# Moving modulation loads and half of the query and key stores to other DMA queues in a two-layer transformer kernel

## The chip, the cores and the metric

The kernel runs on one core of one Trainium2 chip. The metric is device time in microseconds (us). The kernel before took 3096.09 us, the median of 3 runs (3091.0 to 3099.82). The core has five engines that run side by side, each with its own instruction queue in a fixed order: TensorE (PE, matrix products; its weight loads are shown as PEld), VectorE (DVE), ScalarE (ACT), GpSimd (POOL) and SyncE (SP). A transfer between memory and the core's on-chip buffers is issued by an instruction in one of these queues and then runs by itself; an instruction that needs its data waits for it on a semaphore, and everything behind that instruction on the same engine waits too.

## The reference

Two transformer layers over 1024 tokens and 256 context tokens of width 1024, in float32. Only the beginning of the first layer matters here:

```
mod   = silu(c)     @ mod_w[0] + mod_b[0]      # 6 x 1024 numbers: shifts, scales and gates
mod_c = silu(c_ctx) @ mod_w[0] + mod_b[0]
xn = rms_norm(h,  norm1_g) * (1 + sc1)  + sh1
cn = rms_norm(hc, norm1_g) * (1 + csc1) + csh1
aq, ak, av, bq, bk, bv = split(xn @ w_in)      # the same for cn
aq, ak, bq, bk = apply_rope(...)               # pairs (x1, x2) -> (x1 cos - x2 sin, x1 sin + x2 cos)
```

Attention, a convolutional feed-forward network, and a second layer with gated linear attention follow. The shifts sh2, scales sc2 and gates g1, g2 of layer 0 are not needed before the attention's output.

## The kernel before

Products in float32 are made of three products of split operands: `split` (L104) writes the rounded high part with ScalarE (`wh`, L110) and the rest with VectorE (`wl`, L90, the line of the helper `tt`).

The stage that is changed is `attn_in` (from L344). After norming, the queries and keys are made in six pairs of projections: `part(w0)` gives the even channels E of 4 heads for all 1280 tokens, `part(w0 + 1)` the odd channels O. Each is 120 matrix products into one of the two accumulators `big`, so the next projection but one can't start before VectorE and ScalarE have emptied the accumulator. Emptying means: multiply with cosines and sines (`ec`, `es` for E; `os`, `oc` for O), and split the 256 context columns as they are (`shi`, `slo`, L110 and L90, 128x256). From the four products come the two rotated halves, which are split again (128x1024) and stored to DRAM as 4 blocks of 32 rows, 1280 columns each: four stores of 640 KB for a pair, a high and a low one for each rotated half. The stores are issued by GpSimd (L100, `dma2`). The tiles `shi` and `slo` have two buffers each, so a pair's context split waits for the stores of the pair before. The last key projection (`ks[2]`, L456 to L459) makes four stores of 2 blocks of 32 rows, 320 KB each.

Between the projections the rest of the modulation of layer 0 is worked in: 32 blocks of 128 rows of `mod_w` (transposed), 512 KB each. `mod_block` (L300) loads one into the tile `mraw` (two buffers here) and VectorE reduces it twice at L308, against the rows of silu(c) and silu(c_ctx), 1.2 us a pass (`junk` is the first pass, `mraw` the second). The load of a block can be issued once the block two before it has been reduced. `some_mod(n)` takes the next n blocks.

All loads are issued by SyncE (L96, `dma`): the modulation blocks as well as the weights (`wraw`, two buffers, 512 KB each). Three engines' orders are not written by hand in this stage: a scheduler puts the recorded instructions of each engine in one order by its own estimate of when each can run. So VectorE's order mixes emptying, weight splits (`wl`) and modulation passes, and it changes when a transfer moves to another queue.

Of the kernel before, what the change touches and what calls it, by code (L numbers as in the profile page):

```python
# [9 lines left out]
F32 = mybir.dt.float32  # L10
# [34 lines left out]
class K:  # L45
# [254 lines left out]
    def mod_block(self, pool, src, dst, rows):  # L300

        raw = pool.tile([P, 1024], F32, name="mraw", tag="mraw", bufs=self.mbufs)
        self.dma(raw, src)
        for v, row in enumerate(rows):
            out = raw
            if v < len(rows) - 1:
                out = pool.tile([P, 1024], mybir.dt.bfloat16, name="junk", tag="junk", bufs=1)
            self.nc.vector.tensor_tensor_reduce(out=out, in0=raw, in1=row, scale=1.0, scalar=0.0,  # L308
                                                op0=ALU.mult, op1=ALU.add, accum_out=dst[:, v:v + 1])
# [38 lines left out]
    def attn_in(self, esv):  # L348
        nc, io = self.nc, self.io
        with ExitStack() as esx:  # L350
            es0 = ExitStack()
            hp = self.pool(es0, "x0")
            x = [hp.tile([P, T], F32, name=f"x0{k}") for k in range(KD)]
            mp = self.pool(es0, "mod0")
            xp = self.pool(esx, "xn1", side="right")
            xh = [xp.tile([P, T], F32R, name=f"x1h{k}") for k in range(KD)]
            xl = [xp.tile([P, T], F32R, name=f"x1l{k}") for k in range(KD)]
            self.open_tmp()
            xs = lambda k, a, b: x[k][:, a:a + b]
            A, B = self.A[0][0], self.B[0][0]  # L360

            def load_x(t0, n):
                for k in range(KD):
                    self.dma(x[k][:, t0:t0 + n], io["xT"][k, :, t0:t0 + n])

            load_x(*MAIN0)
            self.mbufs = 3
            rows = self.mod_rows(xp, 2)
            y = self.rstd_rows(xs, *MAIN0, True)
            first = [self.mod_first(mp, rows, lambda: self.load_w(io["w_qk"][0])), self.load_w(io["w_qk"][1])]  # L370
            load_x(*MAIN1)
            for k in range(KD):
                self.norm_chunk(k, xs, xh, xl, *MAIN0, A[:, :, 0], B[:, :, 0], y)
            self.norm_mod(xs, xh, xl, *MAIN1, A[:, :, 0], B[:, :, 0], True)
            load_x(*CTX)
            self.norm_mod(xs, xh, xl, *CTX, A[:, :, 1], B[:, :, 1], True)
            self.close_tmp()
            es0.close()
            vp = self.pool(esv, "v")
            fh = lambda k, a, b: xh[k][:, a:a + b]  # L380
            fl = lambda k, a, b: xl[k][:, a:a + b]
            with ExitStack() as es1:
                rp = self.pool(es1, "rope")
                cos = rp.tile([P, NM], F32, name="cos")
                sin = rp.tile([P, NM], F32, name="sin")
                self.dma(cos, io["cos"])
                self.dma(sin, io["sin"])
                self.mbufs = 2
                mod = []

                def some_mod(n):
                    if not mod:
                        mod.append(self.mod_steps([(0, j) for j in (2, 3, 4, 5)], rows, rp))
                    for _ in range(n):
                        next(mod[0], None)

                def full(name, bufs):
                    return rp.tile([P, NM], F32, name=name, tag=name, bufs=bufs)

                def halves():  # L400
                    return [rp.tile([P, T], F32R, name="s" + a, tag="s" + a, bufs=2) for a in ("hi", "lo")]

                def part(j):
                    ps = self.big()
                    self.proj(ps, first[j] if j < 2 else self.load_w(io["w_qk"][j]), fh, fl, TALL)
                    return ps

                M, C = slice(0, NM), slice(NM, T)

                def pair(w0, scr):  # L410

                    def out(eo, t):
                        hi, lo = hl[eo]
                        self.split(hi[:, M], lo[:, M], t)
                        for half, y in ((0, hi), (1, lo)):
                            r = 64 * half + 32 * eo
                            self.dma2(scr[:, r:r + 32, :], y.bitcast(F32))
                    hl = [halves(), halves()]
                    E = part(w0)
                    ec, es, oc, os = (full(a, 1) for a in ("ec", "es", "oc", "os"))  # L420
                    self.tt(ec, E[:, M], cos, ALU.mult)
                    self.tt(es, E[:, M], sin, ALU.mult)
                    self.split(hl[0][0][:, C], hl[0][1][:, C], E[:, C])
                    some_mod(2)
                    O = part(w0 + 1)
                    self.tt(os, O[:, M], sin, ALU.mult)
                    self.tt(oc, O[:, M], cos, ALU.mult)
                    self.split(hl[1][0][:, C], hl[1][1][:, C], O[:, C])
                    self.tt(ec, ec, os, ALU.subtract)
                    out(0, ec)  # L430
                    self.tt(es, es, oc, ALU.add)
                    out(1, es)
                    some_mod(2)

                self.vA = vp.tile([P, 10, P], F32, name="vA")
                self.vB = [[vp.tile([P, 5, 256], F32, name=f"vB{g}{b}") for b in range(2)] for g in range(2)]

                def values(g):
                    self.proj_tok([io["w_v"][2 * g], io["w_v"][2 * g + 1]], fh, fl, self.vB[g], 10)
                    some_mod(2)  # L440
                for j in range(6):
                    pair(2 * j, self.qs[j] if j < 4 else self.ks[j - 4])
                    if j == 3:
                        values(0)

                E = part(12)
                hi, lo = halves()
                ec, es = full("ec", 1), full("es", 1)
                self.tt(ec, E[:, M], cos, ALU.mult)
                self.tt(es[0:64], E[64:128, M], sin[64:128], ALU.mult)  # L450
                self.tt(es[64:128], E[0:64, M], sin[0:64], ALU.mult)
                self.split(hi[:, C], lo[:, C], E[:, C])
                self.tt(ec[0:64], ec[0:64], es[0:64], ALU.subtract)
                self.tt(ec[64:128], ec[64:128], es[64:128], ALU.add)
                self.split(hi[:, M], lo[:, M], ec)
                for half, y in ((0, hi), (1, lo)):  # L456
                    for eo in range(2):
                        r = 64 * half + 32 * eo
                        self.dma2(self.ks[2][:, r:r + 32, :], y[64 * eo:64 * eo + 64].bitcast(F32))  # L459
                some_mod(4)  # L460

                E = part(13)
                vt = halves()[0].bitcast(F32)
                nc.scalar.copy(vt, E[:, :T])
                for b0, nb in ((0, 4), (4, 4), (8, 2)):
                    ps = self.sm()
                    for b in range(nb):
                        nc.tensor.transpose(out=ps[:, b * P:(b + 1) * P], in_=vt[:, (b0 + b) * P:(b0 + b + 1) * P],
                                            identity=self.ident)
                    nc.scalar.copy(self.vA[:, b0:b0 + nb, :], ps[:, :nb * P].rearrange("p (b e) -> p b e", e=P))  # L470
                self.attn_consts(vp)
                values(1)
                some_mod(48)

    def proj_tok(self, srcs, fh, fl, dst, nblk):

# [1357 lines left out]
```

## Time and profile before

| | |
|---|---|
| median of 3 runs | 3096.09 us (3091.0 to 3099.82) |
| profiled execution, its own time | 3087.69 us |
| its span | 3085.8 us |
| mean granted clock of TensorE | 0.982 of full speed |
| TensorE busy | 2931.9 us (95%) |
| VectorE busy | 2272.7 us (74%) |
| ScalarE busy | 1486.7 us (48%) |
| GpSimd busy | 82.7 us (3%) |

The profiled execution is 8.4 us under the median of the runs (0.27%), so a sum is made against 3087.69 us and the difference is carried over to the median. Busy shares are means over stages with different limits. The changed stage lies between 75 us and 330 us of the span, and what a change there is worth has to be read from that stretch.

### The profile page before, as it was taken

The page shows a single profiled execution, that of the slowest core. Times are in us where ns is not written, and L with a number is a line of the kernel's source. Part 1 is how long each engine was busy: PE and PEld are TensorE (multiplying, and loading weights), DVE is VectorE, ACT ScalarE, POOL GpSimd, SP SyncE. Part 2 cuts the span into 40 slices and gives each one's busy share as a digit, 9 for nine tenths or more (in the row PEclk, how much of TensorE's full clock was granted, in tenths as well). Part 3 has the DMA queues.
Part 4 walks back from the last instruction along what each step waited for, and adds up shares of the span by engine and source line. Part 5 has one row for each costly group of instructions (what it writes and reads, how often), then busy time and mean ns, then how long its engine had stood idle before and what let it go on. Part 6 is the DMA issues. An engine that isn't in the chain of part 4 may idle for free.

```text
span 3085.8 us, 41864 instructions
## 1 busy us (share of the span) xinstructions
PE 2931.9 (95%) x15758; PEld 2469.0 (80%) x15758; DVE 2272.7 (74%) x3805; ACT 1486.7 (48%) x2720; POOL 82.7 (3%) x148
## 2 busy tenths in 40 slices
PE   8888799999999999999998999999999899999997
PEld 4687789998898788887887888888877688887886
DVE  7666388887598888887876568688687988887454
ACT  5111277776466544445354355445454544445342
POOL 0000000000000000000000000000000000000000
PEclk9989899999999999999999999999999999999999
DMA  6664652211555322223856651111143222225552
GB/s 217 187 180 140 159 150 63 62 56 51 196 165 187 110 82 82 82 81 130 298 176 194 210 183 36 45 42 46 44 166 123 75 82 82 82 82 191 177 171 90
DMA packets 185443, 383.95 MB, mean 124 GB/s; under 512 B 28276, under 2 KB 89588, under 8 KB 185240
## 3 DMA queue, kind: packets, MB, share of 16 engines
q1 hardware_dynamic: 159032, 326.70, 33.2%
q0 software_dynamic: 25056, 52.48, 5.5%
q8 instruction: 124, 2.03, 0.3%
q10 hardware_dynamic: 1152, 2.10, 0.2%
q14 instruction: 79, 0.65, 0.1%
HBM read 311.44 MB, written 69.73 MB: 124 GB/s over the span
## 4 chain that ended last, share of the span: by engine, by line
PE 73%; DVE 10%; issue 7%; DMA 5%; ACT 4%; POOL 1%; SPq 0%; DVEq 0%; ACTq 0%; POOLq 0%
PE bk L1053 26%; PE bk L1138 16%; PE big L140 14%; DMA mraw<-in_mod_wt_dram 3%; PE sm L553 2%; PE sm L602 2%; PE sm L668 2%; PE big L487 2%; PE big L528 2%; PE sm L1635 2%; PE big L536 2%; PE sm L1566 1%; DVE F L90 1%; DMA wraw<-in_ffn_down_dram 1%; DVE wl L90 1%
## 5 line engine op out<-in xcount | busy, mean ns | idle before, releaser
L110 ACT CAST wh<-wraw 128x512 fp32r<-128x512 f32 x568 | 345.8, 619 | 699.4 <-PE bk L1138 205.4
L90 DVE TENSOR_TENSOR wl<-wraw,wh 128x512 fp32r<-128x512 f32 x568 | 387.9, 687 | 297.8 <-ACT wh L110 277.9
L1138 PE MATMUL bk<-dh,wh 128*128 128x512 f32 (+1 forms) x880 | 328.8, 374 | 15.3 <-ACT wh L110 10.9
L1138 PE MATMUL bk<-dl,wh 128*128 128x512 f32 (+1 forms) x880 | 326.9, 371 | 3.8 <-DVE dl L90 3.8
L1138 PE MATMUL bk<-dh,wl 128*128 128x512 f32 (+1 forms) x880 | 326.8, 371 | 0.2 <-DVE wl L90 0.2
L110 ACT CAST wh<-S 128x512 fp32r<-128x512 f32 x176 | 108.9, 621 | 225.6 <-DVE S L90 118.3
L1138 PEld LDWEIGHTS bk<-dh,wh 128*128 128x128 f32 x880 | 168.2, 191 | 46.8 <-ACT wh L110 11.7
L1138 PEld LDWEIGHTS bk<-dl,wh 128*128 128x128 f32 x880 | 168.3, 191 | 33.2 <-DVE dl L90 4.7
L1138 PEld LDWEIGHTS bk<-dh,wl 128*128 128x128 f32 x880 | 168.2, 191 | 28.3 <-DVE wl L90 0.9
L140 PE MATMUL big<-x1h,wh 128*128 128x512 f32 (+1 forms) x336 | 124.1, 372 | 23.5 <-DVE slo L90 22.5
L308 DVE CUSTOM_DVE_ANT_0 mraw<-mraw,crow 128x1024 f32<-128x1024 f32 x88 | 107.5, 1221 | 31.7 <-DMA mraw<-in_mod_wt_dram 30.6
L140 PE MATMUL big<-x1h,wl 128*128 128x512 f32 (+1 forms) x336 | 124.9, 372 | 5.9 <-DVE wl L90 5.9
L90 DVE TENSOR_TENSOR wl<-S,wh 128x512 fp32r<-128x512 f32 x176 | 120.1, 684 | 11.1 <-ACT wh L110 10.8
L140 PE MATMUL big<-x1l,wh 128*128 128x512 f32 (+1 forms) x336 | 124.3, 371 | 0.0
L87 DVE SCALAR_TENSOR_TENSOR h<-h,cw,h 128x1023 f32<-128x1023 f32 x88 | 111.0, 1279 | 17.9 <-ACT h L93 17.8
L87 DVE SCALAR_TENSOR_TENSOR hh<-hh,cw,hh 128x1023 f32<-128x1023 f32 x88 | 110.9, 1278 | 15.5 <-ACT hh L93 15.4
L560 ACT COPY wt<-sm 128x512 f32<-128x512 f32 (+1 forms) x196 | 95.7, 527 | 38.6 <-PE sm L553 38.2
L308 DVE CUSTOM_DVE_ANT_0 junk<-mraw,crow 128x1024 bf16<-128x1024 f32 x56 | 68.4, 1221 | 55.1 <-DMA mraw<-in_mod_wt_dram 54.8
L553 PE MATMUL sm<-ident,pt 128*128 128x128 f32 x672 | 103.7, 277 | 5.3 <-DVE oc L723 3.3
L584 DVE TENSOR_REDUCE nm<-big 128x1 f32<-128x1280 f32 x64 | 95.4, 1490 | 18.0 <-PE big L536 17.9
L140 PE MATMUL bk<-x2ch,wh 128*128 128x256 f32 x352 | 101.0, 287 | 3.9 <-ACT wh L110 3.0
L140 PE MATMUL big<-x3h,wh 128*128 128x512 f32 x256 | 103.9, 406 | 0.0
(468 smaller groups left out, 8249.4 us busy)
## 6 DMA issues: line engine op xcount, KB each, us to landing
wraw<-in_ffn_down_dram SPq DMA_DIRECT2D x110, 512.0 KB, 3.9
mraw<-in_mod_wt_dram SPq DMA_DIRECT2D x88, 512.0 KB, 4.3
wraw<-in_ffn_up_dram SPq DMA_DIRECT2D x88, 512.0 KB, 3.5
graw<-in_ffn_up_dram SPq DMA_DIRECT2D x44, 512.0 KB, 3.5
dx<-gs SPq DMA_DIRECT2D x88, 256.0 KB, 4.4
gs<-h POOLq DMA_DIRECT2D x22, 512.0 KB, 2.9
gs<-hh POOLq DMA_DIRECT2D x22, 512.0 KB, 2.9
q<-qs SPq DMA_DIRECT2D x40, 256.0 KB, 3.3
```

The lines of the kernel that those rows point to most:

```text
L87: return self.nc.vector.scalar_tensor_tensor(out=out, in0=in0, scalar=scalar, in1=in1, op0=op0, op1=op1)
L90: return self.nc.vector.tensor_tensor(out=out, in0=a, in1=b, op=op)
L110: self.nc.scalar.copy(hi, src)
L140: self.nc.tensor.matmul(ps[:, t0:t0 + n], self.columns(a, k * m, m), b(k, t0, n), start=(k == 0 and j == 0), stop=(k == KD - 1 and j == 2))
L308: self.nc.vector.tensor_tensor_reduce(out=out, in0=raw, in1=row, scale=1.0, scalar=0.0, op0=ALU.mult, op1=ALU.add, accum_out=dst[:, v:v + 1])
L487: self.nc.tensor.matmul(ps[:, 256 * b:256 * b + 256], a(k, t0, P), self.columns(w, k % 4 * 256, 256), start=(k == 0 and j == 0), stop=(k = ...
L528: nc.tensor.matmul(out, q[:, 0, s, :], key, start=True, stop=False)
L553: nc.tensor.transpose(out=ps[:, b * P:(b + 1) * P], in_=self.p[:, (b0 + b) * P:(b0 + b + 1) * P], identity=k.ident)
L560: copy(self.wt[:, b0 * P:(b0 + c) * P], self.tp[g][:, :c * P])
L584: nc.vector.tensor_reduce(out=nm, in_=self.S[m][:, :T], axis=AX.X, op=ALU.max, negate=True)
L1053: nc.tensor.matmul(ps, a[:, s], b, start=(start and k == 0 and j == 0), stop=(k == 3 and j == 2), skip_group_check=True)
L1138: nc.tensor.matmul(out(d), self.columns(a, d * P, P), b, start=(c == 0 and j == 0 and d % per == 0), stop=(c == NFF - 1 and j == 2), skip_ ...
```

## The change

Three transfers change their queue, in the stage between the opening of `rope` and the end of `attn_in` alone:

- the 32 loads of modulation blocks go from SyncE's queue to GpSimd's (`mod_dma2`, set after the sines and cosines are loaded, and unset at the end of the stage);
- the stores of the high parts `shi` (12 of 640 KB, 2 of 320 KB) go from GpSimd's queue to ScalarE's, each behind the ScalarE copy that made its data;
- the stores of the low parts `slo` stay in GpSimd's queue.

What is computed, the sizes of the transfers, the buffers and the memory layout stay as they are.

```
     def mod_block(self, pool, src, dst, rows):
         raw = pool.tile([P, 1024], F32, name="mraw", tag="mraw", bufs=self.mbufs)
-        self.dma(raw, src)
+        (self.dma2 if self.mod_dma2 else self.dma)(raw, src)
...
-            self.mbufs = 3
+            self.mbufs, self.mod_dma2 = 3, False
...
-                self.mbufs = 2
+                self.mbufs, self.mod_dma2 = 2, True
...
                         for half, y in ((0, hi), (1, lo)):
                             r = 64 * half + 32 * eo
-                            self.dma2(scr[:, r:r + 32, :], y.bitcast(F32))
+                            (self.dma2 if half else nc.scalar.dma_start)(scr[:, r:r + 32, :], y.bitcast(F32))
...
-                        self.dma2(self.ks[2][:, r:r + 32, :], y[64 * eo:64 * eo + 64].bitcast(F32))
+                        (self.dma2 if half else nc.scalar.dma_start)(self.ks[2][:, r:r + 32, :], y[64 * eo:64 * eo + 64].bitcast(F32))
...
                 some_mod(48)
+                self.mod_dma2 = False
```

GpSimd's queue at the start of the stage, before (`qs_97` to `qs_100` are the scratch arrays of query pairs 0 to 3):

```order
L100 DMA qs_97<-shi 4x32x1280 x2
L100 DMA qs_97<-slo 4x32x1280 x2
L100 DMA qs_98<-shi 4x32x1280
L100 DMA qs_98<-slo 4x32x1280
L100 DMA qs_98<-shi 4x32x1280
L100 DMA qs_98<-slo 4x32x1280
```

and now:

```order
L100 DMA mraw<-in_mod_wt_dram 128x1024 x4
L100 DMA qs_97<-slo 4x32x1280 x2
L100 DMA mraw<-in_mod_wt_dram 128x1024 x6
L100 DMA qs_98<-slo 4x32x1280 x2
L100 DMA mraw<-in_mod_wt_dram 128x1024 x6
L100 DMA qs_99<-slo 4x32x1280 x2
L100 DMA mraw<-in_mod_wt_dram 128x1024 x5
L100 DMA qs_100<-slo 4x32x1280
```

The low stores of a pair now stand in one queue with the modulation loads, two of them ahead of the next six loads. SyncE's queue has only weight loads left in this stage, and ScalarE's queue has 14 stores, each one behind the copy of its data.

VectorE's order where the first pair is emptied (pair 0, the first two modulation blocks of the stage), with what is gone and what is new:

```order
 L90 TENSOR_TENSOR ec<-big,cos 128x1024
-L90 TENSOR_TENSOR wl<-wraw,wh 128x512
+L308 ISA junk,mod<-mraw,crow_243 128x1024
+L308 ISA mod 128x1
 L90 TENSOR_TENSOR es<-big,sin 128x1024
+L308 ISA mraw,mod<-mraw,crow_258 128x1024
+L308 ISA mod 128x1
+L90 TENSOR_TENSOR slo<-big,shi 128x256
```

A modulation block's two passes now stand among the instructions that empty E's accumulator, where a weight split and the first product of O stood.

VectorE's order where the last block of the stage (`mraw_2670`) stands beside the emptying of the fifth pair's E (`big_1737`), before:

```order
L308 ISA mraw_2665,mod_82<-mraw_2665,crow1_258 128x1024
L308 ISA mod_82 128x1
L90 TENSOR_TENSOR wl_2058<-wraw_2055,wh_2057 128x512
L308 ISA junk_2672,mod_82<-mraw_2670,crow0_243 128x1024
L308 ISA mod_82 128x1
L90 TENSOR_TENSOR ec_1820<-big_1737,cos_618 128x1024
L90 TENSOR_TENSOR es_1821<-big_1737,sin_619 128x1024
L90 TENSOR_TENSOR wl_2062<-wraw_2055,wh_2061 128x512
L90 TENSOR_TENSOR slo_1734<-big_1737,shi_1733 128x256
```

and now:

```order
L308 ISA mraw_2665,mod_82<-mraw_2665,crow1_258 128x1024
L308 ISA mod_82 128x1
L90 TENSOR_TENSOR wl_2058<-wraw_2055,wh_2057 128x512
L90 TENSOR_TENSOR ec_1820<-big_1737,cos_618 128x1024
L90 TENSOR_TENSOR es_1821<-big_1737,sin_619 128x1024
L90 TENSOR_TENSOR wl_2062<-wraw_2055,wh_2061 128x512
L90 TENSOR_TENSOR slo_1734<-big_1737,shi_1733 128x256
L308 ISA junk_2672,mod_82<-mraw_2670,crow0_243 128x1024
L308 ISA mod_82 128x1
```

The first pass of the last block has moved from ahead of this emptying to behind it.

## Rows read from the trace of the kernel before

**Rows 1.** Chain that ended last within the first 420 us, shares by line
```profile
by line: PE big L140 24.7%; DMA mraw<-in_mod_wt_dram 21.3%; PE big L487 6.4%; DVE mraw L308 4.5%; PE sm L158 4.1%; DVE junk L308 3.7%; issue 3.7%; DMA q<-qs 2.8%; DMA mt<-in_mod_w_dram 2.7%; DVE slo L90 2.1%; SPq L96 2.1%; DVE wl L90 1.9%; 
```

**Rows 2.** TensorE's waits, 75 to 265 us (total us, times, longest)
```profile
PE big L140 <- DVE slo L90: 22.5, 5, 12.4
PE big L140 <- DVE wl L90: 5.9, 1, 5.9
PE big L487 <- DVE slo L90: 3.8, 2, 3.0
```

**Rows 3.** Busy us of engines by stretch, then PEclk, DMA share, GB/s
```profile
core 0: us, PE busy (x) PEld busy (x) DVE busy (x) ACT busy (x) POOL busy (x), PEclk, DMA share, GB/s
75.00:265.00 190.00, 157.87 (x861) 137.23 (x861) 133.33 (x209) 28.09 (x46) 11.05 (x16) 0.92 0.62 179
159.20:164.90 5.70, 5.68 (x14) 4.46 (x15) 5.67 (x11) 0.00 (x0) 0.00 (x0) 0.50 0.44 126
193.10:199.00 5.90, 5.90 (x28) 5.90 (x29) 3.59 (x5) 0.00 (x0) 0.00 (x0) 0.50 0.50 162
```

**Rows 4.** Timeline of VectorE: start, us, instruction [idle before <-releaser]
```profile
81.24 1.22 DVE L90 TENSOR_TENSOR ec<-big,cos 128x1024 f32<-128x1024 f32 x1
85.24 0.41 DVE L90 TENSOR_TENSOR slo<-big,shi 128x256 fp32r<-128x256 f32 x1
...
115.39 1.22 DVE L308 CUSTOM_DVE_ANT_0 junk<-mraw,crow 128x1024 bf16<-128x1024 f32 x1 [11.36 <-DMA mraw<-in_mod_wt_dram]
...
157.50 1.23 DVE L308 CUSTOM_DVE_ANT_0 junk<-mraw,crow 128x1024 bf16<-128x1024 f32 x1 [13.96 <-DMA mraw<-in_mod_wt_dram]
158.65 0.08 DVE L308 DVE_READ_ACCUMULATOR2_ANT mod<- 128x1 f32 x1
158.65 0.42 DVE L90 TENSOR_TENSOR slo<-big,shi 128x256 fp32r<-128x256 f32 x1
...
192.51 0.42 DVE L90 TENSOR_TENSOR slo<-big,shi 128x256 fp32r<-128x256 f32 x1 [6.79 <-DMA qs<-slo]
194.80 1.22 DVE L308 CUSTOM_DVE_ANT_0 junk<-mraw,crow 128x1024 bf16<-128x1024 f32 x1 [1.86 <-DMA mraw<-in_mod_wt_dram]
...
231.89 1.22 DVE L308 CUSTOM_DVE_ANT_0 junk<-mraw,crow 128x1024 bf16<-128x1024 f32 x1 [12.23 <-DMA mraw<-in_mod_wt_dram]
```

**Rows 5.** Timeline of GpSimd: the last store of each query pair
```profile
97.68 0.68 POOL L100 DMA_DIRECT2D qs<-slo  x1 [0.46 <-DVE slo L90]
...
136.31 0.68 POOL L100 DMA_DIRECT2D qs<-slo  x1
...
177.75 0.68 POOL L100 DMA_DIRECT2D qs<-slo  x1 [0.93 <-DVE slo L90]
...
215.13 0.68 POOL L100 DMA_DIRECT2D qs<-slo  x1 [0.39 <-DVE slo L90]
```

**Rows 6.** DMA issues: count, KB each, median us to landing
```profile
ks<-shi POOLq DMA_DIRECT2D x4, 640.0 KB, 13.8
...
gs<-h POOLq DMA_DIRECT2D x22, 512.0 KB, 2.9
...
hs<-h SPq DMA_DIRECT2D x8, 512.0 KB, 2.9
...
ks<-shi POOLq DMA_DIRECT2D x2, 320.0 KB, 12.0
```

**Rows 7.** The first store of pair 2 alone, issued at 174.0 us
```profile
L100 POOL DMA_DIRECT2D qs<-shi x1: 680/680/680, 174.0 to 174.0; - x1
...
DMA to landing us min/median/max: 12.4/12.4/12.4
```

**Rows 8.** The stage's first modulation load, issued at 77.0 us
```profile
L96 SPq DMA_DIRECT2D mraw<-in_mod_wt_dram x1: 351/351/351, 77.0 to 77.0; - x1
...
DMA to landing us min/median/max: 6.6/6.6/6.6
```

**Rows 9.** Modulation loads away from stores, 230.5 to 252 us
```profile
L96 SPq DMA_DIRECT2D mraw<-in_mod_wt_dram x6: 327/328/328, 234.4 to 250.4; - x6
...
DMA to landing us min/median/max: 3.4/3.5/3.5
```

**Rows 10.** Waits of all engines, 225 to 265 us
```profile
ACT wh L110 <- DMA wraw<-in_w_qk_dram: 24.0, 1, 24.0
```

**Rows 11.** ScalarE's issues of transfers, ns each (at the kernel's end)
```profile
L1425 ACTq DMA_DIRECT2D out_dram<-hh x8: 338/338/375, 2959.7 to 3081.8; - x8
```

## The prediction

> **What bounds the kernel now.** I read the chain of waits of the first 420 us first. Loads of modulation blocks hold 21.3% of it, as much as the projections do (24.7%) [rows 1]. TensorE's waits show the price: between 75 and 265 us it stood still 32.2 us (22.5 + 5.9 + 3.8), nearly all for `slo` on VectorE, that is, for an accumulator to be emptied [rows 2]. Over these 190 us TensorE was busy 157.87 us and VectorE 133.33 us [rows 3], so neither is full. VectorE's timeline says why: it is idle 11.36, 13.96 and 12.23 us for a modulation block, and the `slo` that TensorE needs stands right behind the block, as at 157.50 and 158.65 us [rows 4]. Each of these blocks is the first whose load was issued behind a pair's stores. From the pair's last store [rows 5] to the pass over that block [rows 4] it takes 115.39 - 97.68 = 17.7 us, 157.50 - 136.31 = 21.2, 194.80 - 177.75 = 17.1 and 231.89 - 215.13 = 16.8, mean 18.2; I call this the gap. Loads away from stores land in 3.5 us [rows 9].
>
> A stall costs TensorE a second time: after two of them its granted clock is 0.50 for 5.7 and 5.9 us [rows 3], the lower of its two levels (1.2 instead of 2.4 GHz), about 2.9 us of work each.
>
> Why the stores take so long: 640 KB in 4 blocks of 32 rows land after 13.8 us, 320 KB in 2 blocks after 12.0 us, but 512 KB in 128 rows after 2.9 us [rows 6]. Half the bytes take nearly the same time, so it goes by the 32 rows of one block, served one after the other (about 12 / 32 = 0.38 us a row), with blocks side by side.
>
> **The change, part by part**, in the time of the profiled execution (3087.69 us, 8.4 us under the median).
>
> *The gap.* Now 4 stores of a pair are ahead of a load, in another queue than it. Then its two low stores are ahead of it in its own queue, and the two high ones run beside it in ScalarE's. The trace shows no load behind stores in one queue, so I bound the gap. From below: 3.5 us, an unhindered load. From above: three such stores one after the other on the same paths, 3 x 12.4 [rows 7] + 1.5 = 38.7 us. I take 14 us, from the nearest row, a store with no other ahead of it (12.4 us [rows 7]), plus about 1.5 us for the load's own 8 rows behind it. That is 3.7, 7.2, 3.1 and 2.8 us less in the four query pairs, together 16.8 us. They count in full where TensorE waits for that very block (pairs 1 and 3); in pairs 0 and 2 they bring VectorE's later work forward, which is the chain there too, and in pair 2 the low store that `slo` waits 6.79 us for [rows 4] lands sooner as well.
>
> *The start of the stage.* The first load, issued at 77.0 us, landed after 6.6 us [rows 8]; from GpSimd the issue takes 0.68 us [rows 5] instead of 0.35, so it lands about 84.0 us. VectorE's new order wants the block right behind `ec`, at 82.4 us [rows 4]. Then the first pass, `es` and the second pass, about 1.14 us each from start to start, put `slo` at 87.4 us instead of 85.24: 2.2 us later, and TensorE with it.
>
> *Stores behind a modulation pass.* In pairs 1 and 3 the second low store now has one pass or a pass and a weight split ahead of it on VectorE, 1.2 and 1.8 us: 3.0 us.
>
> *Passes moved behind.* Near 245 and 264 us a weight split and the fifth pair's `slo`, which end TensorE's last two stalls, each have one pass of 1.2 us less ahead of them: a gain of 2.4 us.
>
> *GpSimd's issue.* The run of nine blocks after pair 3 is set by loads. Their landing is not longer from GpSimd than from SyncE (2.9 against 2.9 us for 512 KB [rows 6]), but the issue is 0.68 against 0.33 us [rows 5, 9]: 9 x 0.35 = 3.1 us lost. Bounds: 0 if the issue hides, and 9 us if each load is 1 us later.
>
> *Cost at nothing.* ScalarE issues 14 transfers at 0.34 us [rows 11], 4.7 us, besides 28.09 us busy of 190 [rows 3]; they are hidden by its idle time, and would cost at most these 4.7 us if that cover were gone. SyncE's weight loads no longer queue behind modulation loads: ScalarE's wait of 24.0 us for one [rows 10] goes, but what TensorE needs from it still stands behind VectorE's passes, so I book nothing. The key stores after 265 us have one load behind them; nothing.
>
> Sum: 16.8 - 2.2 - 3.0 + 2.4 - 3.1 = 10.9 us gained. What is late next is again the first block behind the stores, with a shorter stall, so I leave the half-clock time as it is. 3087.7 - 10.9 = 3076.8; on the median 3096.1 - 10.9 = 3085.2, so I say 3085.
>
> **Rivals.**
>
> *A. The load lands when it did.* Bytes of stores and loads are the same and run at the same time; if they share one capacity, the gap stays 18.2 us. For: at 75 to 265 us the transfers are busy 0.62 of the time on average [rows 3]. Against: only the store's 32 rows in a line are slow, not the volume. Then 16.8 us drop out: 5.9 us slower, 3102. The Trainium skill has this as a rule (DMA: Bandwidth & Descriptors, "Issuing engines are not separate DMA queues": all queues end on the same 16 engines and only issue time is saved); whether it holds for the gap no row here shows.
>
> *B. High stores pile up (the slower side).* If both high stores of ScalarE's queue are served on the same four paths, one behind the other, they take 2 x 12.4 = 24.8 us [rows 7] from the first issue, 3.5 us ahead of the last low store: a gap of 21.3 us or more, since a load needs every path. Where a low store lands on these four too, it waits its turn, and the gap is 24.8 + 1.5 = 26.3 us. Say 26.3 in pairs 0 and 2, 21.3 in 1 and 3: 8.6 + 9.2 + 0.1 + 4.5 = 22.4 us lost instead of 16.8 gained, 28.3 us slower in full; TensorE's slack in pairs 0 and 2 (it waited little there) takes perhaps half, so 3112. It decides from a mean gap of about 16.7 us, where the sum is zero (16.8 us over four pairs is 4.2 each, and the rest costs 5.9). For: a store by four blocks occupies few paths [rows 6]. Against: nothing here shows which paths a queue picks. The Trainium skill names the paths (same page, "Why a DMA increments its semaphore by 16 and not by 1": a hardware queue takes the lowest-numbered k engines, a software queue moves on from a cursor); by it both high stores of every pair would share four engines. No row shows that.
>
> *C. Stalls go altogether.* With a gap near 8 us VectorE keeps ahead, and most of the 32.2 us of stalls and some half-clock time go: about 30 to 38 us, 3062. For: VectorE has 57 us idle in 190. Against: a low store alone already takes 12.4 us.
>
> **How the numbers follow.** The forecast has a chance of 0.42 and reaches from 3074 to 3093; A 0.22 (3094 to 3105), B 0.24 (3100 to 3125), C 0.12 (3055 to 3074). A measurement of this kernel can't tell less than 0.3%, 9.3 us, from no change. Faster than 3086.8: 0.6 of the forecast and all of C, 0.25 + 0.12, and with B or A unlikely to reach it 0.38; I round up to 0.42, as the half-clock time I booked at nothing can only fall with the stalls. Slower than 3105.4: 0.8 of B and a little of A, 0.23. Between them 0.35. The range is 3060 to 3113, which leaves out some of C's and B's far ends.
>
> **What would show it.** In the profile after: the pass over the first block behind each pair's low stores 14 us after the last of them (18 would be A, over 21 B); TensorE's longest stall near 159 us down from 12.4 to 5 or 6 us; the first `slo` of the stage 2 us later than 85.24; 0.68 us for each load on GpSimd; high stores landing 12 to 14 us after their issue, both, where B has the second of a pair at 20 us or more. Wrong would be: VectorE waiting for `mraw` more than before in all, or ScalarE waiting for a store's buffer.

## The result and the profile after

The changed kernel takes 3120.84 us (median of 6 runs, 3117.91 to 3128.79), the kernel before 3093.55 us (6 runs, 3089.23 to 3099.82): 27.3 us slower, a ratio of 1.0088 with a 95% interval of 1.0073 to 1.0102. The forecast of 3085 us was wrong in sign, and the time lies above the range. The profiled execution took 3117.91 us with a span of 3116.0 us, 30.2 us more than that of before; its mean granted clock is 0.978 instead of 0.982.

The loss lies in the changed stage. The first load of a key tile (`kc`), behind the stage's last weight loads in SyncE's queue, is issued at 383.57 us instead of 354.54: 29.0 us later. Over the stretch of [rows 3] TensorE was busy 144.32 us instead of 157.87, and its clock was 0.88 instead of 0.92 (columns as there):

```profile
75.00:265.00 190.00, 144.32 (x789) 125.84 (x787) 111.31 (x173) 25.77 (x41) 19.82 (x34) 0.88 0.49 154
```

TensorE's waits for VectorE in it are 37.3 us instead of the 32.2 us of [rows 2] (us in all, times, longest). The stall that was 12.4 us, in pair 1, is now 10.6; the forecast had 5 or 6. The longest is in pair 2, 12.5 us instead of 3.0:

```profile
PE big L140 <- DVE slo L90: 23.1, 3, 10.6
...
PE big L488 <- DVE slo L90: 14.2, 2, 12.5
```

The gap is read from two timelines, as with [rows 4] and [rows 5]. GpSimd's last low store of each query pair, after (start, us, instruction, idle before):

```profile
97.36 0.72 POOL L100 DMA_DIRECT2D qs<-slo  x1 [2.16 <-DVE slo L90]
...
145.29 0.71 POOL L100 DMA_DIRECT2D qs<-slo  x1 [2.32 <-DVE slo L90]
...
186.94 0.71 POOL L100 DMA_DIRECT2D qs<-slo  x1 [2.17 <-DVE slo L90]
...
232.92 0.72 POOL L100 DMA_DIRECT2D qs<-slo  x1 [0.59 <-DVE slo L90]
```

and VectorE's timeline, after, with the start of the stage and the rows that wait for transfers:

```profile
80.92 1.22 DVE L90 TENSOR_TENSOR ec<-big,cos 128x1024 f32<-128x1024 f32 x1
...
85.47 0.42 DVE L90 TENSOR_TENSOR slo<-big,shi 128x256 fp32r<-128x256 f32 x1
...
122.84 1.23 DVE L308 CUSTOM_DVE_ANT_0 junk<-mraw,crow 128x1024 bf16<-128x1024 f32 x1 [17.47 <-DMA mraw<-in_mod_wt_dram]
...
163.93 1.23 DVE L308 CUSTOM_DVE_ANT_0 junk<-mraw,crow 128x1024 bf16<-128x1024 f32 x1 [12.03 <-DMA mraw<-in_mod_wt_dram]
...
208.03 0.42 DVE L90 TENSOR_TENSOR slo<-big,shi 128x256 fp32r<-128x256 f32 x1 [14.21 <-DMA qs<-slo]
...
212.79 1.23 DVE L308 CUSTOM_DVE_ANT_0 junk<-mraw,crow 128x1024 bf16<-128x1024 f32 x1 [4.33 <-DMA mraw<-in_mod_wt_dram]
...
249.97 1.23 DVE L308 CUSTOM_DVE_ANT_0 junk<-mraw,crow 128x1024 bf16<-128x1024 f32 x1 [14.94 <-DMA mraw<-in_mod_wt_dram]
...
322.47 0.42 DVE L90 TENSOR_TENSOR slo<-big,shi 128x256 fp32r<-128x256 f32 x1 [14.61 <-DMA ks<-slo]
```

The gaps are 122.84 - 97.36 = 25.5 us, 163.93 - 145.29 = 18.6, 212.79 - 186.94 = 25.9 and 249.97 - 232.92 = 17.1, together 87.1 us, where [rows 4, 5] gave 72.8. (In pair 3 the load stands between the two low stores in GpSimd's queue; it is issued at 231.78 us.) The gaps alternate from pair to pair. So does the time from issue to landing of the low stores. In the kernel before it was (one answer for each query pair, two stores in each)

```profile
DMA to landing us min/median/max: 17.8/19.1/20.4
...
DMA to landing us min/median/max: 14.6/17.8/21.0
...
DMA to landing us min/median/max: 16.9/18.9/20.9
...
DMA to landing us min/median/max: 15.7/17.4/19.1
```

and is now

```profile
DMA to landing us min/median/max: 24.2/24.5/24.7
...
DMA to landing us min/median/max: 17.4/17.6/17.8
...
DMA to landing us min/median/max: 23.9/24.3/24.6
...
DMA to landing us min/median/max: 17.2/17.4/17.5
```

In pairs 1 and 3 they land as they did, in pairs 0 and 2 some 5 us later.

A second place lost time that the prediction had at nothing: the wait at 322.47 us for a key store. VectorE's waits from 75 to 400 us, before (us in all, times, longest):

```profile
DVE junk L308 <- DMA mraw<-in_mod_wt_dram: 45.9, 12, 14.0
DVE slo L90 <- DMA qs<-slo: 6.8, 1, 6.8
DVE slo L90 <- DMA ks<-slo: 2.6, 2, 1.5
```

and after:

```profile
DVE junk L308 <- DMA mraw<-in_mod_wt_dram: 63.0, 14, 17.5
DVE slo L90 <- DMA ks<-slo: 17.9, 2, 14.6
DVE slo L90 <- DMA qs<-slo: 14.2, 1, 14.2
```

VectorE's wait for loads in all, 63.0 instead of 45.9 us, is the sign that the prediction named for being wrong. The gaps are 14.3 us longer in all, and the waits for key stores 17.9 - 2.6 = 15.3 us. That this sum, 29.6 us, is close to the 29.0 us by which the stage ends later is luck: a wait can also take the place of idle time that was there before. Where the time went is read from the starts of two products on VectorE, the first of the fifth pair (a key pair) and the first of `ks[2]`, before

```profile
261.30 1.22 DVE L90 TENSOR_TENSOR ec<-big,cos 128x1024 f32<-128x1024 f32 x1
...
309.83 1.22 DVE L90 TENSOR_TENSOR ec<-big,cos 128x1024 f32<-128x1024 f32 x1 [0.20 <-PE big L140]
```

and after:

```profile
284.96 1.22 DVE L90 TENSOR_TENSOR ec<-big,cos 128x1024 f32<-128x1024 f32 x1
...
338.87 1.22 DVE L90 TENSOR_TENSOR ec<-big,cos 128x1024 f32<-128x1024 f32 x1 [0.20 <-PE big L140]
```

The pass behind pair 3's stores starts 249.97 - 231.89 = 18.1 us later, the fifth pair 23.7 us and `ks[2]` 29.0 us. So 18.1 us were lost in the query pairs, 5.6 us in the run of modulation blocks behind them, and 5.4 us in the key pairs. The key store's wait of 14.6 us cost less than that: in the kernel before VectorE stood idle at the same place too, 8.25 us for a weight (`wh`).

The last view shows who used the 16 DMA engines between 94 and 99 us, when the two high stores of the first pair were under way and the low ones had moved no data yet (packets, MB, share of the 16):

```profile
q10 hardware_dynamic: 64, 0.33, 23.5%
```

Queue q10 is ScalarE's; the view counts it and SyncE's q1 as hardware queues and GpSimd's q0 as a software queue. Two stores in flight and no more than 23.5% of the engines' time: that is the share of four engines of sixteen (25%). In the kernel before, with the four stores of this pair all from GpSimd's queue, the answer for 99 to 104 us is

```profile
q0 software_dynamic: 178, 0.91, 98.1%
```

so there the stores lay on all sixteen. This is what rival B needed and what no row ahead of the prediction showed. The landing of the high stores themselves, which the prediction named as a sign, stands in no view.

### The profile page after: what moved, and what is told of

It is laid out like the page before. It is cut to its first block, busy times and chain, and to the rows that moved or that the text cites. A ratio compares the mean times of both kernels' runs of the same rounds, so it can differ in the third digit from the quotient of the medians.

```text
span 3116.0 us, 41845 instructions
## 1 busy us (share of the span) xinstructions
PE 2938.4 (94%) x15758; PEld 2472.5 (79%) x15758; DVE 2273.3 (73%) x3805; ACT 1488.2 (48%) x2720; POOL 91.1 (3%) x166
## 4 chain that ended last, share of the span: by engine, by line
PE 69%; issue 14%; DVE 9%; ACT 3%; DMA 3%; POOL 1%; SPq 1%; POOLq 0%; DVEq 0%; ACTq 0%
PE bk L1054 26%; PE bk L1139 15%; PE big L140 11%; PE sm L554 2%; PE sm L603 2%; PE big L488 2%; PE sm L669 2%; PE big L529 2%; PE sm L1636 2%; PE big L537 2%; PE sm L1567 1%; DVE F L90 1%; DVE hh L87 1%; DMA wraw<-in_ffn_down_dram 1%; DMA ks<-slo 1%
## 5 line engine op out<-in xcount | busy, mean ns | idle before, releaser
L1139 PE MATMUL bk<-dh,wh 128*128 128x512 f32 (+1 forms) x880 | 329.5, 374 | 15.9 <-ACT wh L110 11.5
L140 PE MATMUL big<-x1h,wl 128*128 128x512 f32 (+1 forms) x336 | 125.9, 375 | 10.9 <-DVE wl L90 10.9
L90 DVE TENSOR_TENSOR wl<-S,wh 128x512 fp32r<-128x512 f32 x176 | 120.5, 686 | 11.3 <-ACT wh L110 11.2
L87 DVE SCALAR_TENSOR_TENSOR h<-h,cw,h 128x1023 f32<-128x1023 f32 x88 | 111.0, 1280 | 17.9 <-ACT h L93 17.8
L585 DVE TENSOR_REDUCE nm<-big 128x1 f32<-128x1280 f32 x64 | 95.4, 1491 | 17.9 <-PE big L537 17.8
L140 PE MATMUL bk<-x2ch,wl 128*128 128x256 f32 x352 | 101.7, 289 | 3.0 <-DVE wl L90 2.8
```

What stands on the lines that cost most here:

```text
L87: return self.nc.vector.scalar_tensor_tensor(out=out, in0=in0, scalar=scalar, in1=in1, op0=op0, op1=op1)
L90: return self.nc.vector.tensor_tensor(out=out, in0=a, in1=b, op=op)
L140: self.nc.tensor.matmul(ps[:, t0:t0 + n], self.columns(a, k * m, m), b(k, t0, n), start=(k == 0 and j == 0), stop=(k == KD - 1 and j == 2))
L585: nc.vector.tensor_reduce(out=nm, in_=self.S[m][:, :T], axis=AX.X, op=ALU.max, negate=True)
L1139: nc.tensor.matmul(out(d), self.columns(a, d * P, P), b, start=(c == 0 and j == 0 and d % per == 0), stop=(c == NFF - 1 and j == 2), skip_ ...
```

## The experiments

Three things changed at once: the queue of the stores, that of the loads, and with them VectorE's order. The theories: *pile-up* (the high stores of a pair share the same four paths), *FIFO* (loads suffer since they stand behind low stores in GpSimd's queue), *order* (VectorE's new order is what costs). Diffs are against the changed kernel unless said otherwise; each time stands against runs of the kernel before on the same chip (medians 3091.45 to 3093.23 us). How far an order differs is counted on VectorE's timelines, from the first `ec` of the stage to the last of `ks[2]`: of 169 instructions 17 stand elsewhere in the changed kernel than before.

**Stores split, loads back on SyncE** (`e1_stores_only`).

```
-                self.mbufs, self.mod_dma2 = 2, True
+                self.mbufs, self.mod_dma2 = 2, False
```

> Only the stores are split over two queues (high parts from ScalarE, low parts from GpSimd); the modulation loads stay in SyncE's queue as before. Pile-up theory (both high stores of a pair share the same four paths, one behind the other): the gap from a pair's last low store to the pass over the first block behind it stays at 25 us in two of the four pairs and 17 in the others, and the time is 3108 to 3121 us, most of the 27 us that were lost. FIFO theory (what costs is that loads stand behind low stores in GpSimd's queue): gaps at or under the 17 us of the kernel before and 3085 to 3096 us. Order theory (VectorE's new order costs): VectorE's order is nearly the old one, so 3090 to 3097 us.

Measured: 3109.56 us, ratio 1.0061 (1.0043 to 1.0079). So most of the loss is there without a single load behind a store. The low stores' landings, pairs 0 to 3:

```profile
DMA to landing us min/median/max: 26.1/27.0/27.9
...
DMA to landing us min/median/max: 20.5/21.3/22.1
...
DMA to landing us min/median/max: 26.4/26.8/27.2
...
DMA to landing us min/median/max: 18.7/19.5/20.2
```

and VectorE's waits for stores of `slo`, 75 to 400 us:

```profile
DVE slo L90 <- DMA qs<-slo: 29.1, 3, 17.6
...
DVE slo L90 <- DMA ks<-slo: 15.6, 2, 12.8
```

The time of the pile-up theory came, by another way than it said. The loads, in a queue of their own, overtake the low stores (gaps of 12.4, 15.1 and 13.3 us in pairs 0, 1 and 3), but the low stores themselves land at least as late as in the changed kernel, and the next pair's context split waits for their buffer: 29.1 + 15.6 = 44.7 us, against 6.8 + 2.6 before. On the order theory this time decides nothing: VectorE's order was expected to be nearly the old one, but 13 instructions stand elsewhere than before, and 17 elsewhere than in the changed kernel.

**Loads on GpSimd, all stores there as before** (`e2_loads_only`).

```
-    (self.dma2 if half else nc.scalar.dma_start)(scr[:, r:r + 32, :], y.bitcast(F32))
+    self.dma2(scr[:, r:r + 32, :], y.bitcast(F32))          # and the same for ks[2]
```

> Only the modulation loads move to GpSimd's queue; all stores stay in GpSimd's queue as before. Pile-up theory: the four stores of a pair lie on all 16 paths side by side as before, so the gaps are 17 to 21 us as before and the time 3090 to 3104 us (the load's later issue and VectorE's order may cost a few us). FIFO theory: four stores of a pair are now ahead of the loads in one queue, gaps of 22 us or more, 3110 to 3125 us. Order theory: VectorE's order is that of the changed kernel, so 3112 to 3121 us with gaps as before.

Measured: 3104.72 us, 1.0040 (1.0025 to 1.0054), 0.7 us above what pile-up allowed and 5 us under the FIFO theory's lower end. The order theory's figure stood on VectorE's order being that of the changed kernel, and it isn't (23 instructions stand elsewhere, 28 against the kernel before), so it is not decided here either. The first pair's last store and the pass behind it, on GpSimd's timeline

```profile
98.19 0.68 POOL L100 DMA_DIRECT2D qs<-slo  x1 [0.89 <-DVE slo L90]
```

and VectorE's

```profile
120.10 1.22 DVE L308 CUSTOM_DVE_ANT_0 junk<-mraw,crow 128x1024 bf16<-128x1024 f32 x1 [5.22 <-DMA mraw<-in_mod_wt_dram]
```

give a gap of 21.9 us; the others are 21.5, 22.4 and 19.1, 12.1 us more than before in all, beside 13.3 us measured. So a load behind the stores in one queue waits longer than beside them in another, by 3 us a pair in the mean. How much of the 13.3 us this is, the run can't say, as VectorE's order changed as well; the time is about half of what the FIFO theory asked for. The two halves alone cost 18.1 and 13.3 us and together 27.3 us.

**The same bytes, block by block** (`e3_after_blocks`): the changed kernel, with each store of 4 blocks of 32 rows issued as four stores of 32 rows (2 for `ks[2]`), in the same queues.

```
-    (self.dma2 if half else nc.scalar.dma_start)(scr[:, r:r + 32, :], y.bitcast(F32))
+    for b in range(4):
+        (self.dma2 if half else nc.scalar.dma_start)(scr[b, r:r + 32, :], y[32 * b:32 * b + 32].bitcast(F32))
```

> The changed kernel, but each store of 4 (2) blocks of 32 rows is issued as 4 (2) stores of one block of 32 rows each, in the same queue; its outermost dimension is then 32 rows, so that a store should use all 16 paths. Same bytes, same queues. Pile-up theory: no store is bound to four paths any more, a pair's stores (2.6 MB) land 7 to 10 us after the last issue, the gaps fall under 12 us in all pairs and the time to 3055 to 3085 us, below the kernel before. FIFO theory: the loads still stand behind the low stores, but these land sooner: gaps of 12 to 18 us, 3085 to 3105 us. Order theory: 3112 to 3121 us.

Measured: 3052.2 us, 0.9878 (0.9861 to 0.9894): faster than both kernels, 39 us under the one before. Low stores land after 2.4 to 6.0 us. Its waits from 75 to 400 us, with all that TensorE waited for VectorE:

```profile
DVE junk L308 <- DMA mraw<-in_mod_wt_dram: 12.8, 7, 3.5
...
PE big L140 <- DVE slo L90: 4.9, 1, 4.9
```

TensorE is busy 185.10 of the 190 us of [rows 3], at a granted clock of 0.99:

```profile
75.00:265.00 190.00, 185.10 (x1042) 160.87 (x1041) 143.06 (x214) 37.13 (x59) 35.38 (x70) 0.99 0.62 192
```

VectorE's order is not that of the changed kernel (46 of 159 instructions stand elsewhere), so the 67 us between the two need not be the stores' alone.

**The kernel before, block by block, all in GpSimd's queue** (`e4_before_blocks`; the same edit on the kernel before).

> The kernel before, with each store of 4 (2) blocks issued as 4 (2) stores of one block of 32 rows, all in GpSimd's queue, the modulation loads in SyncE's. GpSimd then issues 16 stores for a pair, at about 0.5 to 0.7 us each 8 to 11 us. Pile-up theory: the stores of a pair already lay on all 16 paths, so spreading them gains only the serial service of 32 rows by one path: gaps of 8 to 14 us, 3065 to 3088 us. FIFO theory says nothing of this kernel's loads: it gives the same time as before, 3090 to 3097 us, unless the 32 rows in a line set the gap. Order theory: VectorE's order is the old one, 3090 to 3097 us.

Measured: 3079.03 us, 0.9957 (0.9942 to 0.9972). The gaps are 5.9, 4.5, 5.6 and 5.5 us, shorter than the 8 to 14 expected. So stores that already used all paths gain too when they are written block by block. With the blocks the change's sign turns round: its moves make 3079 us into 3052, VectorE's order moving along again.

**Only the high stores block by block** (`e5_high_blocks`).

```
+    if half:
+        self.dma2(scr[:, r:r + 32, :], y.bitcast(F32))
+    else:
+        for b in range(4):
+            nc.scalar.dma_start(scr[b, r:r + 32, :], y[32 * b:32 * b + 32].bitcast(F32))
```

> The changed kernel with only the high stores (ScalarE's queue) issued block by block, so that they no longer stay on four paths; the low stores stay at 4 blocks in GpSimd's queue, with the modulation loads behind them. Pile-up theory: the high stores are gone within some 5 us, a low store stands alone on its four paths and lands after 12 to 15 us in every pair (24, 18, 24, 17 in the changed kernel), the gap is the 14 to 16 us that the prediction had, the alternation between pairs goes, and the time is 3075 to 3092 us. Rival (the low store itself, with the loads behind it, is what takes 17 to 25 us, whatever the high stores do): gaps as in the changed kernel, 3110 to 3121 us.

Measured: 3117.74 us, 1.0078 (1.0064 to 1.0092): against the pile-up theory. The landings are nearly as it said, 11.2 to 16.9 us in the query pairs. But the order is another: the scheduler put the second low store behind two loads. GpSimd's timeline, both low stores of pair 0:

```profile
95.33 0.72 POOL L100 DMA_DIRECT2D qs<-slo  x1 [4.34 <-DVE slo L90]
...
115.59 0.72 POOL L100 DMA_DIRECT2D qs<-slo  x1 [14.33 <-DVE slo L90]
```

VectorE waits for a block behind each of them, up to 112.92 and 128.88 us. Two gaps in a pair (17.6 and 13.3 us) follow each other where the changed kernel has one of 25 us in every other pair. So this run decides nothing by its time.

**The same, with GpSimd's order held** (`e9_high_blocks_order`): the eight high stores of a pair are written behind the second copy, and GpSimd's queue is again word for word the changed kernel's through the query and key pairs. VectorE's order is not: 18 of 167 instructions stand elsewhere than in the changed kernel, about as many as between that and the kernel before.

```
+                            if half:
+                                self.dma2(scr[:, r:r + 32, :], y.bitcast(F32))
+                        for e in range(2 * eo):
+                            for b in range(4):
+                                nc.scalar.dma_start(scr[b, 32 * e:32 * e + 32, :], hl[e][0][32 * b:32 * b + 32].bitcast(F32))
```

> The kernel with only the high stores block by block (3117.7 us) had another order than the changed kernel: two modulation loads stand between the two low stores of a pair, so each low store delays a load of its own (passes 17.6 and 13.3 us behind them in the first pair). Here the same block-by-block high stores are written behind the copy of the second half; GpSimd's queue is then word for word that of the changed kernel, with the two low stores together. Pile-up theory: low stores land after 12 to 16 us in all pairs, the gap is 14 to 17 us once a pair instead of 25.5, 18.6, 25.9 and 17.1, the waits of a context split for a key store (17.9 us in the changed kernel) fall under 5 us, and the time is 3080 to 3100 us. Rival (the high stores' paths don't matter, only the queue that the loads stand in): 3112 to 3121 us with gaps as in the changed kernel.

Measured: 3093.33 us, 1.0002 (0.9993 to 1.0012): the loss is gone. GpSimd's last low stores

```profile
98.22 0.72 POOL L100 DMA_DIRECT2D qs<-slo  x1 [2.15 <-DVE slo L90]
...
136.21 0.71 POOL L100 DMA_DIRECT2D qs<-slo  x1 [2.32 <-DVE slo L90]
```

and VectorE's passes behind them, pairs 0 and 1,

```profile
114.43 1.23 DVE L308 CUSTOM_DVE_ANT_0 junk<-mraw,crow 128x1024 bf16<-128x1024 f32 x1 [8.55 <-DMA mraw<-in_mod_wt_dram]
...
150.96 1.23 DVE L308 CUSTOM_DVE_ANT_0 junk<-mraw,crow 128x1024 bf16<-128x1024 f32 x1 [9.22 <-DMA mraw<-in_mod_wt_dram]
```

give gaps of 16.2 and 14.8 us (pairs 2 and 3: 16.8 and 15.6), the alternation is gone, low stores of the query pairs land after 13.2 to 17.2 us, and the waits for key stores are 6.6 us (under 5 was expected). Between 95 and 99 us ScalarE's queue now holds 79.9% of the engines' time instead of a quarter:

```profile
q10 hardware_dynamic: 244, 0.79, 79.9%
```

**Only the low stores block by block** (`e6_low_blocks`; the loop of e5 on the other half).

> The changed kernel with only the low stores issued block by block; the high stores stay at 4 blocks in ScalarE's queue. Pile-up theory: the first four paths are still taken for about 25 us a pair; each low store has 2 of its 32 rows of a block on every path, so it and the loads share those paths row by row with the high stores but are not bound to them: low stores land after 4 to 8 us, gaps of 6 to 13 us, the same in all pairs, time 3060 to 3085 us. Rival (high stores alone hold the loads until they are done, since a load needs every path): gaps of 21 us or more, 3105 to 3121 us.

Measured: 3088.93 us, 0.9986 (0.9976 to 0.9995), between the two theories, as are its numbers. Low stores land after 6 to 17 us, not 4 to 8. The first load behind them is issued only 7.9 us after the last low store's first block (106.53 against 98.61 us) and lands 13.0 us later, so the first pass stands 119.53 - 98.61 = 20.9 us behind that block, near what the rival said; the time is not the rival's. Between 114 and 119 us ScalarE's queue still holds 12.5% of the engines' time. So with spread low stores a load still takes 13.0 us beside piled high ones, where 3.5 us is what it takes away from stores [rows 9]; the run doesn't split the loss further, since VectorE's order differs in 43 of 157 instructions.

**The suspected cost doubled** (`e7_high_halves`): each high store as two stores of 2 blocks.

```
+    for b in (0, 2):
+        nc.scalar.dma_start(scr[b:b + 2, r:r + 32, :], y[32 * b:32 * b + 64].bitcast(F32))
```

> The changed kernel with each high store of the queries and keys (640 KB, 4 blocks) issued as two stores of 2 blocks, both in ScalarE's queue. Pile-up theory with the lowest-numbered paths: a store of 2 blocks takes the first two paths only, four such stores of a pair follow each other there, 4 x 12.4 = 50 us of service for a pair that lasts 43 us; only 2 paths are taken by the high stores, and the stage becomes slower by 10 us or more a pair: 3180 to 3300 us. Rival (stores of one queue land side by side, each in some 12 us whatever its form, or a queue moves on to the next paths): the four halves lie side by side, 3105 to 3125 us.

Measured: 3165.75 us, 1.0237 (1.0223 to 1.0251). It lies 14 us under the lower end that pile-up gave and 41 us above the rival's upper one. From 96 to 101 us two and then three of a pair's four stores are under way from ScalarE's queue and the fourth is being issued, and the view of the DMA queues has

```profile
q10 hardware_dynamic: 32, 0.16, 11.5%
```

half the packets and half the share of the changed kernel: the share of two engines of sixteen (12.5%).

**The second high store from SyncE's queue** (`e10_high_two_queues`), with VectorE's and GpSimd's orders unchanged.

```
-    (self.dma2 if half else nc.scalar.dma_start)(scr[:, r:r + 32, :], y.bitcast(F32))
+    (self.dma2 if half else self.dma if eo else nc.scalar.dma_start)(scr[:, r:r + 32, :], y.bitcast(F32))
```

> The changed kernel, but the second high store of each query and key pair is issued from SyncE's queue instead of ScalarE's; VectorE's and GpSimd's orders are unchanged. If every hardware queue serves a store of 4 blocks on the same four paths (the lowest-numbered), the two high stores still take about 25 us together, low stores land after 24 and 17 us as in the changed kernel, and the time is 3112 to 3125 us. Rival (the stores pile up only because they follow each other in one queue, and two queues use different paths): low stores after 12 to 18 us in all pairs, 3085 to 3105 us.

Measured: 3131.16 us, 1.0122 (1.0108 to 1.0136), 6 us above the upper end of the pile-up theory; the rival falls. The low stores' landings, pairs 0 to 3:

```profile
DMA to landing us min/median/max: 26.5/27.2/27.9
...
DMA to landing us min/median/max: 19.9/20.1/20.2
...
DMA to landing us min/median/max: 27.8/28.0/28.2
...
DMA to landing us min/median/max: 16.6/16.7/16.7
```

The high stores thus pile up from two hardware queues as from one. Since both orders are unchanged, this is the cleanest of the runs on that point. Why it is 10 us slower than the changed kernel stays open; ScalarE waits 54.1 us for weight loads of the queries and keys here instead of 29.1, and these loads now stand behind a store on SyncE.

**All stores block by block, loads on SyncE** (`e8_blocks_loads_sp`).

> All stores block by block, high parts from ScalarE and low parts from GpSimd, the modulation loads back in SyncE's queue. If loads behind low stores still cost something when the stores are short, this beats the kernel with all stores in blocks and the loads on GpSimd (3052 us): 3040 to 3050 us. If the weight loads gain more from an empty SyncE queue, or VectorE's order decides, it is slower than that one: 3053 to 3065 us.

Measured: 3058.26 us, 0.9891 (0.9877 to 0.9904). No better than e3: with short stores no gain is seen from taking the loads out of their queue, though VectorE's order differs here too. e3 is the fastest version found.

## Why the prediction was wrong, point by point

**What bounds the kernel**: right in the main. How late a pair's stores land decides the stage: e3, where they land after 2.4 to 6.0 us, has hardly a stall. It reaches VectorE by the gap or, as e1 shows, by the wait for the stores' buffer.

**The gap** is the step that failed: "I take 14 us, from the nearest row, a store with no other ahead of it". The low store has no other ahead of it in its queue, but it has on its paths. Between the bounds of 3.5 and 38.7 us that row answered for a store with nothing ahead of it on its paths [rows 7], and nothing in it said that the low store would have that. With the high stores spread over all paths (e9) the gaps are 16.2, 14.8, 16.8 and 15.6 us, near the 14 forecast; with them piled up they are 25.5, 18.6, 25.9 and 17.1. The term was a gain of 16.8 us and came out as a loss of 14.3. Its mechanism was written down, as rival B: 26.3 us in pairs 0 and 2 was right to within 0.8 us, and 21.3 in pairs 1 and 3 was 2.7 and 4.2 too much. The halving ("TensorE's slack in pairs 0 and 2 takes perhaps half") was wrong: pair 2's gap grew by 8.8 us, and VectorE's delay against the kernel before grew with it from 8.0 us at the next pair's `ec` to 16.7 us at its `os`. It was also wrongly carried out, as half of 8.6 + 9.2 us leaves 3115.5 and not 3112. In full B gave 3096.1 + 28.3 = 3124.4 us, 3.6 from the measured median; that is luck in part, since its gaps were 8.1 us too long in all and the run behind pair 3 and the key pairs cost more than it had.

The Trainium skill names the paths (DMA: Bandwidth & Descriptors, "Why a DMA increments its semaphore by 16 and not by 1": a hardware queue uses the lowest-numbered k engines, the software queue goes on from a cursor). The traces agree with it at three points: 23.5% of the engines for stores of 4 blocks, 11.5% for stores of 2, and the same pile-up from two hardware queues. By it the alternation would follow as well: two low stores of 4 blocks move the cursor on by eight of sixteen, and so meet the lowest four in every other pair. No run shows the cursor, nor which engines by number, and why both low stores of such a pair land late stays open.

B had 0.24 and the forecast 0.42, on the ground that "nothing here shows which paths a queue picks". That is a reason for even odds between the two.

**Key stores behind 265 us**, "nothing": VectorE waits 15.3 us more for them, and the key pairs lose 5.4 us. The step looked at what stands behind the store in its queue (one load) and not at who waits for its buffer. In the changed kernel the key pairs' low stores land after 16.9 to 24.6 us, which two buffers of `slo` don't cover; in the kernel before, after 13.2 to 17.3 us in the first key pair, they did but for 2.6 us.

**The start of the stage**: 2.2 us forecast. From `ec` to `slo` it took 85.47 - 80.92 = 4.55 us instead of 85.24 - 81.24 = 4.00 [rows 4], 0.55 us. The two passes were added and the weight split and the product that left the same place were not taken off. VectorE also found the block there at 82.05 us without a wait, where the prediction had it land at 84.0.

**GpSimd's issue**: the issue of a load takes 0.53 to 0.59 us there, not the 0.68 of a store [rows 5], yet the run behind pair 3 cost more than the 3.1 us booked, 5.6 us. Nine loads are issued 3.6 us apart (252.77 to 281.77 us), before eight 3.2 us apart (234.4 to 256.6), which is about 4 us in nine. They land after 3.6 to 5.1 us, where [rows 9] had 3.5, so the judgement that landing is not longer from GpSimd, made on stores of another stage [rows 6], was wrong here. One pass more of 1.2 us stands in the run.

**Stores behind a pass** (3.0 lost): right. From `os` to the split that the last low store waits for it is 7.9 us instead of 6.1 in pair 1 and 7.8 instead of 6.6 in pair 3. **Passes moved behind** (2.4 gained): no gain is seen; the two stalls of 5.9 and 3.2 us became 10.9 and 4.7. e9 shows what the terms behind the gaps weigh together. Its gaps are 63.4 us in all, 9.4 less than before, and the pass behind pair 3's stores starts at 226.86 us, 5.0 earlier than before; but from there to the fifth pair's first product it takes 37.6 us instead of 29.4, so that run eats the gain.

**ScalarE's issues**, 0.34 us each and hidden: 0.53 us, 1.11 for the first; with 25.77 us busy of 190 ScalarE had the time for them, as forecast.

**The half-clock time** left as it is: the granted clock of the stretch fell from 0.92 to 0.88 with the longer stalls, so this was an error in the same direction as the gap.

**The other rivals**: A (the gap stays as it was) is out, since the gap moved both ways with the layout of the stores. VectorE's new order as a cost of its own is not excluded: no run has the changed kernel's order without the pile-up. What it can explain is small beside the 18.1 us of the query pairs, where VectorE waits for transfers that land later, but it may have a part in the 5.6 us behind them. C's mechanism was not reached by the change, but e3 shows that it exists and what it is worth: 39 us, when the stores become short (30 to 38 were forecast for it).

## What to carry to other kernels

Ask of every transfer which of the 16 DMA paths it uses, not only which queue it is in: here a store whose outermost dimension is 4 had the share of four paths, and from hardware queues such stores piled up on each other, from one queue or two. Try stores with a longer outermost dimension (here 32 rows instead of 4 blocks: 3079 instead of 3091 us, and 3052 with the change on top). And where a scheduler sets the order, compare the orders before believing a time: e5 and e9 have the same high stores, block by block, and differ by 24 us.

## What the runs showed of the hardware that was not expected

A software queue and a hardware queue treat the same store differently: four 640 KB stores from GpSimd's hold 98.1% of the engines' time, two from ScalarE's 23.5%.

An issue can hold its engine for long. In e7 ScalarE's third and fourth store of the first pair take 8.36 us to issue, 7.50 of them the fourth (start, us, instruction):

```profile
97.28 8.36 ACTq L421 DMA_DIRECT2D qs<-shi  x2
```

and seven short ones in a row in e9 take 5.79 us, 0.83 each, where one of four blocks takes 0.53 in the changed kernel. What the issue waits for there no view shows.
